# A decoder layer on one core: v is brought to token order by block transposes on VectorE and transfers through DRAM, in place of TensorE's transposes

## The chip, the cores and the metric

The kernel runs on one core of a Trainium2 chip. The metric is the device time of one execution in microseconds (us). Times are compared as medians of several runs. The engines are named as the profile names them: PE is TensorE (PEld its weight loads), DVE is VectorE, ACT is ScalarE, POOL is GpSimd, SP is SyncE, whose queue issues all of this kernel's DMAs.

## What is computed

One layer of a hybrid decoder, on a prompt of 2048 tokens of width 1024 and on 8 samples of 4 tokens. After a layer norm and a modulation, one wide projection gives u, v, z of a gated MLP, q, k, v of a gated DeltaNet with 8 heads of 128, and gates. The change is in the DeltaNet branch:

```
qkv_c, conv_new = _short_conv(qkv, conv_buf, conv_w)      # 4 taps along the tokens, then silu
q, k, v = jnp.split(qkv_c, 3, axis=-1)
q = _l2norm(q.reshape(B, L, H_B, DK)); k = _l2norm(k.reshape(B, L, H_B, DK)); v = v.reshape(B, L, H_B, DV)
...
a_mat = jnp.where(strict, einsum('bhnid,bhnjd->bhnij', kb, k) * decay, 0.0)
lhs = a_mat + jnp.eye(C)
u = triangular_solve(lhs, vb); w = triangular_solve(lhs, kb * exp(gc))
...
def step(S, xs):                                          # chunk after chunk
    v_new = u_n - w_n @ S
    o = (q_n * exp(gc_n)) @ S + qk_n @ v_new
    S = S * exp(g_last) + (k_n * exp(g_last - gc_n)).T @ v_new
```

So a head's v is needed with tokens as rows, scaled token by token, when the head's recurrence over the chunks of tokens begins.

## The kernel before

**Tiling.** The prompt runs in two halves of 1024 tokens. A projection computes 128 output columns ("group") for all tokens of a half, with channels on the 128 partitions and tokens along the free dimension: three pieces of 384, 384 and 256 + 32 sample tokens in the first half (CG[0]), two of 512 in the second (CG[1]). Each f32 operand is split into a high and a low fp32r part, so a piece is 8 x 3 matmuls on PE (project, line 906, matmuls recorded by mm at line 438). In each half come, for each of 8 heads, the groups k, q, v, z_b and for six heads a gate g_a; then the other groups.

**From a projection to the recurrence.** qkv_sink (line 1178) takes a piece of k, q or v out of PSUM into a buffer of the role "cp" (two of them, x0 the first half, y the second), does the convolution and silu, and starts k_token, q_token or v_token. These bring the piece to token order: v_token (line 1336) waits for the factor vf from k_token, transposes each chunk of 128 tokens on PE by tp (recorded at line 443) into a PSUM bank of the role "pt" (three banks), frees the buffer, and multiplies by vf on DVE into KV, the buffer of the head's k and v in token order (the tile Y4F or Y5F, by turns; tt, line 404). When all pieces are there, "vs" is signalled, for which chain (line 1523) waits.

**The inverse.** gram (line 1370) forms the products of k and q on PE. inverse (line 1412) sends their 32x32 diagonal blocks through DRAM (d_blk: four writes, four reads), POOL inverts them in 62 short steps (line 407), the result goes through DRAM again (d_td), DVE transposes 32x32 blocks (line 1446), and PE combines them to 128x128 inverses (lines 1470 to 1509). Then chain runs its eight chunks one after another, with DVE and ACT steps between its matmuls.

**What sets the order.** Every instruction is recorded by a planner (Sched): each piece of work is a generator that asks for an engine with an estimated duration and a time from which it can start; the planner takes the one with the least start plus a price by priority, and the engines run the lists in that order, each strictly in its own. A DMA is planned with 475 ns of SP and a transfer time from its bytes. The main stream of projections has the lowest priority and fills PE. A waiting instruction holds up all that stand behind it on its engine or queue. PE's weights are loaded a group or more ahead (wload, line 847).

Of the kernel before, what the change touches and what calls it, by code (L numbers as in the profile page):

```python
# [11 lines left out]
ALU = mybir.AluOpType  # L12

P = 128
D = 1024
KT = 8
H = 8
# [152 lines left out]
def hybrid_step_kernel(ctx: ExitStack, tc: tile.TileContext, x_prompt, x_sample, state_conv, state_ssm,  # L170
# [44 lines left out]
    def V(off, *dims, p0=0, np_=P):  # L215
        dims = [[1, d] if isinstance(d, int) else list(d) for d in dims]
        t, o, st = place(off)
        return bass.AP(t.tensor, t.offset + p0 * st + o, [[st, np_]] + dims)

    def Q(bank, off, *dims, p0=0, np_=P):  # L220
        dims = [[1, d] if isinstance(d, int) else list(d) for d in dims]
        return bass.AP(PS.tensor, PS.offset + p0 * 4096 + bank * 512 + off, [[4096, np_]] + dims)

    def dram(name, n):
        return dr_pool.tile([1, n], F32, name=name)[:]
# [130 lines left out]
    d_blk = [dram(f"d_blk{i}", 32 * 1024) for i in range(2)]  # L356
    d_td = [dram(f"d_td{i}", 32 * 1024) for i in range(2)]


    def fsz(ap):  # L360
        n = 1
        for s in ap.shape[1:]:
            n *= s
        return n
# [52 lines left out]
    def stt(out, a, s, b, op0, op1, dep=None):  # L417
        aps = not isinstance(s, (int, float))
        t = yield ("o", "DVE", dve_ns(out, (a, b)) + 60 * aps, dep)
        nc.vector.scalar_tensor_tensor(out=out, in0=a, scalar=s, in1=b, op0=op0, op1=op1)  # L420
        return t

    def pow_(out, a, which, dep=None):
# [17 lines left out]
    def tp(out, in_, idn=None, dep=None):  # L441
        t = yield ("o", "PE", 109.0, dep)
        nc.tensor.transpose(out, in_, ident[: in_.shape[0], : in_.shape[0]] if idn is None else idn)  # L443
        return t

    def bc(ap, shape):
        return ap.to_broadcast(shape)
# [698 lines left out]
    def hd(half, h):  # L1146
        return heads.setdefault((half, h), {})
# [30 lines left out]
    def qkv_sink(half, s, h):  # L1178
# [13 lines left out]
        def sink(cgi, pb, t):  # L1192
# [33 lines left out]
            t = yield from act(V(x0, n0), y, AF.Tanh, scale=0.5)  # L1226
            if s == 2:
                t = yield from stt(y, V(x0, n0), 1.0, y, ALU.add, ALU.mult)
                S.spawn(v_token(half, h, cgi, xb, t), 1)
            else:  # L1230
                if "KQ" not in me:
                    if "KQw" not in me:
                        me["KQw"] = True
                        kq = yield ("a", "KQ")
                        me["KQ"] = kq
                        S.signal(("KQ", half, h), kq[2])
                ta = yield ("w", ("KQ", half, h))
                dst = V(me["KQ"][0] + (0 if s == 1 else TW) + c0, n0)
                t = yield from stt(dst, V(x0, n0), 1.0, y, ALU.add, ALU.mult, dep=max(t, ta))
                S.release(xb, t)  # L1240
                S.signal(("kq", half, h, s, cgi), t)
                S.spawn(k_token(half, h, cgi, t) if s == 1 else q_token(half, h, cgi, t), 1)
# [91 lines left out]
        S.signal(("vf", half, h, cgi), t)  # L1334

    def v_token(half, h, cgi, yb, t):
        me = hd(half, h)
        ta = yield ("w", ("vf", half, h, cgi))
        cs = chunks(half, cgi)
        m, c0 = len(cs), cs[0]  # L1340
        pb = yield ("a", "pt")
        for i, c in enumerate(cs):
            t = yield from tp(Q(pb[0], i * P, P), V(yb[0] + UNIT + i * P, P), dep=max(t, pb[2]))
        S.release(yb, t)
        vf = V(me["hs"][0] + 16 + 24 + c0, m)
        t = yield from tt(V(me["KV"][0] + TW + c0 * P, [P, m], [1, P]), Q(pb[0], 0, [P, m], [1, P]),
                          bc(vf.unsqueeze(2), [P, m, P]), ALU.mult, dep=max(t, ta))
        S.release(pb, t)
        S.signal(("vs", half, h, cgi), t)

    def q_token(half, h, cgi, t):
# [951 lines left out]
```

## Time and profile before

| | us |
|---|---|
| three runs: lowest, median, highest | 2738.87, 2743.01, 2744.91 |
| the profiled execution | 2741.66 |
| its span, first to last instruction | 2739.8 |
| PE busy | 2692.0 |
| DVE, ACT, POOL busy | 1445.9, 1003.2, 553.5 |

Busy times are unions of an engine's records; matmul records overlap, since they are pipelined. A wait is put down to the instruction whose end released it. The heads of the first half run from about 130 to 760 us, those of the second from about 1480 to 2100 us.

### The profile page before, as it was taken

The numbers are of one execution on the slowest core, as the hardware profiler recorded it, in microseconds if no ns is written. First come the engines' busy times: TensorE is split into PE (matmuls) and PEld (weight loads), VectorE is DVE, ScalarE is ACT, GpSimd is POOL, SyncE is SP. The second block draws the span as 40 slices with busy tenths as digits, with TensorE's granted clock in tenths as the row PEclk, the third lists the DMA queues.
The fourth block names the chain that finished last, engine by engine and source line by source line (L and its number), as shares of the span: only waits on it lengthen the run. The fifth ranks groups of instructions, "written<-read, shape, count | busy, mean of one in ns | idle before, by whom it ended". The sixth has DMA issues, their size and how long they took to land. (4 is left out here: it accounts for less than half of the span.)

```text
span 2739.8 us, 43826 instructions
## 1 busy us (share of the span) xinstructions
PE 2692.0 (98%) x16514; PEld 2362.1 (86%) x16514; DVE 1445.9 (53%) x3194; ACT 1003.2 (37%) x2710; POOL 553.5 (20%) x1452
## 2 busy tenths in 40 slices
PE   6999999999999999999999999999999999999998
PEld 4989989998898999999997888788888888888876
DVE  5677666767552253433547655666663324433446
ACT  5544444545343322221224535444452312222120
POOL 2053444335300000000000443433341000000001
PEclk9999999999999999999999999999999999999999
DMA  6222332222553142233433222222223422233342
GB/s 213 59 70 70 84 90 63 74 69 62 152 190 95 58 125 77 86 111 92 138 109 102 79 77 69 69 61 66 77 59 92 123 95 80 71 114 104 104 124 84
DMA packets 360493, 255.88 MB, mean 93 GB/s; under 512 B 72793, under 2 KB 326033, under 8 KB 360282
## 3 DMA queue, kind: packets, MB, share of 16 engines
q1 hardware_dynamic: 360282, 253.10, 31.3%
q8 instruction: 129, 2.11, 0.3%
q14 instruction: 82, 0.67, 0.1%
HBM read 197.31 MB, written 55.71 MB: 92 GB/s over the span
## 5 line engine op out<-in xcount | busy, mean ns | idle before, releaser
L438 PE MATMUL psum<-TX,TWHL 128*128 128x384 f32 (+3 forms) x9296 | 1981.7, 361 | 3.8 <-DVE TX L404 3.4
L438 PEld LDWEIGHTS psum<-TX,TWHL 128*128 128x128 f32 (+1 forms) x9296 | 1551.8, 188 | 165.1 <-issue 10.8
L395 ACT ACTIVATE arena<-psum 128x128 bf16<-128x128 f32 (+8 forms) x920 | 311.8, 348 | 777.7 <-PE psum L438 620.8
L427 POOL TENSOR_TENSOR arena<-arena 128x1 f32<-128x1 f32 (+4 forms) x139 | 125.4, 903 | 1627.7 <-DVE arena L414 1412.2
L420 DVE SCALAR_TENSOR_TENSOR arena<-arena 128x512 f32<-128x512 f32 (+8 forms) x625 | 344.9, 561 | 92.3 <-ACT arena L395 81.0
L407 POOL TENSOR_TENSOR arena<-arena 128x60 f32<-128x60 f32 (+24 forms) x992 | 343.3, 346 | 132.7 <-DMA arena<-d_blk 26.7
L404 DVE TENSOR_TENSOR TWHL<-arena,TWHL 128x512 fp32r<-128x512 f32 (+1 forms) x344 | 235.4, 689 | 244.0 <-ACT TWHL L395 241.7
L420 DVE SCALAR_TENSOR_TENSOR arena<-arena,psum 128x128 f32<-128x128 f32 (+3 forms) x342 | 132.4, 403 | 361.2 <-PE psum L438 249.8
L395 ACT ACTIVATE TWHL<-arena 128x512 fp32r<-128x512 f32 x344 | 214.8, 627 | 206.8 <-PE psum L438 100.7
L395 ACT ACTIVATE arena<-arena 128x128 f32<-128x128 f32 (+8 forms) x509 | 228.3, 486 | 130.6 <-DVE arena L420 81.3
L443 PE MATMUL psum<-arena 128*128 128x128 f32 (+6 forms) x509 | 126.0, 271 | 2.5 <-ACT Y3F L395 0.8
L404 DVE TENSOR_TENSOR arena<-arena 128x3 f32<-128x3 f32 (+13 forms) x259 | 113.7, 447 | 18.6 <-DMA arena<-d_gc 8.7
L438 PE MATMUL psum<-arena 128*128 128x128 f32 (+6 forms) x524 | 101.6, 293 | 1.0 <-ACT arena L395 1.0
L420 DVE SCALAR_TENSOR_TENSOR arena<-psum,arena 128x512 f32<-128x512 f32 (+4 forms) x80 | 39.9, 510 | 109.8 <-PE psum L438 109.6
L1219 POOL COPY arena<-arena 128x3 f32<-128x3 f32 x120 | 35.8, 298 | 296.8 <-ACT arena L395 296.1
L438 PEld LDWEIGHTS psum<-arena 128*128 128x128 f32 (+5 forms) x524 | 73.8, 163 | 22.4 <-issue 12.7
L443 PEld LDWEIGHTS psum<-arena 128*128 128x128 f32 (+6 forms) x509 | 67.5, 137 | 26.4 <-issue 13.3
L395 ACT ACTIVATE Y7F<-psum 32x256 f32<-32x256 f32 (+6 forms) x115 | 46.6, 406 | 100.2 <-PE psum L438 39.0
L395 ACT ACTIVATE TX<-arena 128x512 fp32r<-128x512 f32 (+2 forms) x84 | 47.1, 586 | 93.1 <-DMA arena<-d_yb 75.7
L395 ACT ACTIVATION_READ_ACCUMULATOR arena<-psum 128x1 f32 (+1 forms) x392 | 76.6, 195 | 0.0
L414 DVE TENSOR_SCALAR arena<-arena 128x3 f32<-128x3 f32 (+10 forms) x234 | 47.6, 211 | 36.0 <-ACT arena L395 24.9
L404 DVE TENSOR_TENSOR TX<-arena,TX 128x512 fp32r<-128x512 f32 (+2 forms) x84 | 52.2, 638 | 24.8 <-ACT TX L395 24.4
(242 smaller groups left out, 2715.2 us busy)
## 6 DMA issues: line engine op xcount, KB each, us to landing
arena<-in_w_in_dram SPq DMA_DIRECT2D x288, 256.0 KB
out_dram<-arena SPq DMA_DIRECT2D x25, 512.0 KB
arena<-in_x_prompt_dram SPq DMA_DIRECT2D x24, 512.0 KB
arena<-d_gc SPq DMA_DIRECT2D x16, 512.0 KB
arena<-d_blk SPq DMA_DIRECT2D x64, 128.0 KB
d_yb<-arena SPq DMA_DIRECT2D x32, 256.0 KB
d_vh<-arena SPq DMA_DIRECT2D x16, 512.0 KB
arena<-d_vh SPq DMA_DIRECT2D x16, 512.0 KB
```

Source lines behind the costliest of these rows:

```text
L395: nc.scalar.activation(out, in_, func, **kw)
L404: nc.vector.tensor_tensor(out=out, in0=a, in1=b, op=op)
L407: nc.gpsimd.tensor_tensor(out=out, in0=a, in1=b, op=op)
L414: nc.vector.tensor_scalar(out=out, in0=a, scalar1=s1, scalar2=s2, op0=op0, **kw)
L420: nc.vector.scalar_tensor_tensor(out=out, in0=a, scalar=s, in1=b, op0=op0, op1=op1)
L427: nc.gpsimd.tensor_tensor(out=out, in0=a, in1=e, op=ALU.pow)
L438: nc.tensor.matmul(out, lhsT, rhs, start=start, stop=stop)
L443: nc.tensor.transpose(out, in_, ident[: in_.shape[0], : in_.shape[0]] if idn is None else idn)
L1219: nc.gpsimd.tensor_copy(V(c_tail + gi, [24, 3]), V(x0 + n0, 3))
```

## The change

v_token no longer uses PE or PSUM. DVE transposes every 32x32 block of a piece within its block of partitions (vtrans), from y back into x0. Four DMAs, one per block of 32 partitions, write the blocks to a DRAM buffer of the piece, d_v, with tokens as rows, in runs of 32 values (128 bytes). One DMA reads it back into KV in rows of 128 values. Then DVE multiplies in place by vf. The buffer "cp" is freed when the writes have landed. The read waits for the buffer KV; the wait for vf comes later than before.

```
+    d_v = {(half, h, i): dram(f"d_v{half}{h}{i}", n * P)
+           for half, ns in enumerate(((384, 384, 256), (512, 512))) for h in range(H) for i, n in enumerate(ns)}
...
+    def vtrans(out, a, dep=None):
+        t = yield ("o", "DVE", fsz(out) / 0.96 + 150, dep)
+        nc.vector.transpose(out, a)
+        return t
...
             if s == 2:
                 t = yield from stt(y, V(x0, n0), 1.0, y, ALU.add, ALU.mult)
+                t = yield from vtrans(V(x0, n0), y)
                 S.spawn(v_token(half, h, cgi, xb, t), 1)
...
     def v_token(half, h, cgi, yb, t):
         me = hd(half, h)
-        ta = yield ("w", ("vf", half, h, cgi))
         cs = chunks(half, cgi)
         m, c0 = len(cs), cs[0]
-        pb = yield ("a", "pt")
-        for i, c in enumerate(cs):
-            t = yield from tp(Q(pb[0], i * P, P), V(yb[0] + UNIT + i * P, P), dep=max(t, pb[2]))
+        dv = d_v[half, h, cgi]
+        for i in range(4):
+            t = yield from dma(DV(dv, 32 * i, [P, 32], [32 * P, 4 * m], [1, 32]),
+                               V(yb[0], [32, 4 * m], [1, 32], p0=32 * i, np_=32), dep=t)
         S.release(yb, t)
+        t = max(t, (yield ("w", ("KV", half, h))))
+        kv = V(me["KV"][0] + TW + c0 * P, [P, m], [1, P])
+        t = yield from dma(kv, DV(dv, 0, [P, P], [P * P, m], [1, P]), dep=t)
+        ta = yield ("w", ("vf", half, h, cgi))
         vf = V(me["hs"][0] + 16 + 24 + c0, m)
-        t = yield from tt(V(me["KV"][0] + TW + c0 * P, [P, m], [1, P]), Q(pb[0], 0, [P, m], [1, P]),
-                          bc(vf.unsqueeze(2), [P, m, P]), ALU.mult, dep=max(t, ta))
-        S.release(pb, t)
+        t = yield from tt(kv, kv, bc(vf.unsqueeze(2), [P, m, P]), ALU.mult, dep=max(t, ta))
         S.signal(("vs", half, h, cgi), t)
```

The planner makes new lists for all engines. Lines of the changed kernel are 3, 9 or 13 higher than those of the kernel before: 378 is 381, 404 is 407, 420 is 423, 438 is 447, 443 is 452, 1446 is 1459, 1470 is 1483.

On PE, in the last piece of the second head's v projection (first half; "128x288" are that piece's matmuls, L443 with psum<-arena the transposes of v, with Y1F those of k), before:

```order
L438 MATMUL psum<-TX,TWHL 128x384 x9
L438 MATMUL psum<-TX,TWHL 128x288 x8
L443 MATMUL psum<-arena 128x128
L438 MATMUL psum<-TX,TWHL 128x288 x4
L443 MATMUL psum<-arena 128x128
L438 MATMUL psum<-TX,TWHL 128x288 x4
L443 MATMUL psum<-arena 128x128
L438 MATMUL psum<-TX,TWHL 128x288 x8
L438 MATMUL psum<-TX,TWHL 128x384 x7
```

and now:

```order
L447 MATMUL psum<-TX,TWHL 128x288 x4
L452 MATMUL psum<-arena,Y1F 128x128
L447 MATMUL psum<-TX,TWHL 128x288 x4
L452 MATMUL psum<-arena,Y1F 128x128
L447 MATMUL psum<-TX,TWHL 128x288
L447 MATMUL psum<-arena 32x128
L447 MATMUL psum<-TX,TWHL 128x288 x10
L447 MATMUL psum<-arena 64x128
L447 MATMUL psum<-TX,TWHL 128x288 x5
L447 MATMUL psum<-TX,TWHL 128x384 x38
```

The three transposes of v are gone from between the projection's matmuls; the last two of the head's k, and two matmuls of the samples, have moved into the piece.

On SP, where the blocks of the fifth head's inverse (first half) go out and come back, before:

```order
L378 DMA arena<-in_w_in_dram 128x4x128 x2
L378 DMA d_blk_78<-Y2F 32x8x32 x4
L378 DMA arena<-d_blk_78 32x1024 x4
L378 DMA d_yb<-arena 128x512
L378 DMA arena<-in_w_in_dram 128x4x128 x2
```

and now:

```order
L381 DMA arena<-in_w_in_dram 128x4x128 x4
L381 DMA d_blk_78<-Y2F 32x8x32 x4
L381 DMA d_yb<-arena 128x32
L381 DMA d_v_94<-arena 32x12x32
L381 DMA arena<-d_blk_78 32x1024 x4
L381 DMA d_v_94<-arena 32x12x32
L381 DMA arena<-in_w_in_dram 128x4x128 x2
L381 DMA d_v_94<-arena 32x12x32
L381 DMA d_yb<-arena 128x512
L381 DMA d_v_94<-arena 32x12x32
```

A write of v, and one of the sample's result, stand between the inverse's writes and its reads, and the other three writes follow among the weight loads.

On DVE, around the first multiply of v by vf in the third head of the second half (TENSOR_TENSOR into Y4F; rows with psum and 128x128 are steps of the second head's chain), before:

```order
L404 TENSOR_TENSOR arena<-psum,arena 128x512
L420 SCALAR_TENSOR_TENSOR arena<-psum,arena,Y5F 128x128
L420 SCALAR_TENSOR_TENSOR Y6F<-Y6F,psum 128x512
L420 SCALAR_TENSOR_TENSOR arena<-arena,psum 128x128
L404 TENSOR_TENSOR Y4F<-psum,arena 128x512
L414 TENSOR_SCALAR arena<-arena 128x4
L420 SCALAR_TENSOR_TENSOR arena<-psum,arena,Y5F 128x128
```

and now:

```order
L423 SCALAR_TENSOR_TENSOR arena<-psum,arena,Y5F 128x128
L407 TENSOR_TENSOR Y0F<-Y0F,arena 128x1024
L407 TENSOR_TENSOR Y4F<-Y4F,arena 128x512
L423 SCALAR_TENSOR_TENSOR Y6F<-Y6F,psum 128x512
L423 SCALAR_TENSOR_TENSOR arena<-arena,psum 128x128
L423 SCALAR_TENSOR_TENSOR arena<-psum,arena,Y6F 128x512
L423 SCALAR_TENSOR_TENSOR arena<-psum,arena,Y5F 128x128
```

The multiply reads Y4F, which a DMA has filled, where it read PSUM; it stands later in the second head's chain, and steps of that chain stand behind it as before.

## Rows read from the trace of the kernel before

**Rows 1.** The page: the span, the engines' busy time, the DMA totals.

```profile
span 2739.8 us, 43826 instructions
PE 2692.0 (98%) x16514; PEld 2362.1 (86%) x16514; DVE 1445.9 (53%) x3194; ACT 1003.2 (37%) x2710; POOL 553.5 (20%) x1452
...
DMA packets 360493, 255.88 MB, mean 93 GB/s; under 512 B 72793, under 2 KB 326033, under 8 KB 360282
...
q1 hardware_dynamic: 360282, 253.10, 31.3%
```

**Rows 2.** Busy time by stage: each engine's us (instructions), PE clock, DMA share.

```profile
130.00:760.00 630.00, 626.45 (x4704) 569.37 (x4703) 428.55 (x1125) 294.45 (x993) 267.44 (x713) 1.00 0.30 83
...
1480.00:2100.00 620.00, 617.00 (x3874) 502.21 (x3873) 372.81 (x745) 283.48 (x828) 231.33 (x622) 1.00 0.26 71
```

**Rows 3.** PE in order of time: start, us from start to last end, instructions.

```profile
170.30 1.23 PE L438 MATMUL psum<-TX,TWHL 128*128 128x288 f32 x8
171.37 0.27 PE L443 MATMUL psum<-arena 128*128 128x128 f32 x1
171.39 0.78 PE L438 MATMUL psum<-TX,TWHL 128*128 128x288 f32 x4
172.01 0.27 PE L443 MATMUL psum<-arena 128*128 128x128 f32 x1
172.04 0.77 PE L438 MATMUL psum<-TX,TWHL 128*128 128x288 f32 x4
```

**Rows 4.** DVE's groups by shape: busy us, mean ns, idle before.

```profile
L1446 DVE STREAM_TRANSPOSE arena<-arena 128x256 f32<-128x256 f32 x16 | 7.0, 438 | 8.8 <-DMA arena<-d_td 8.8
...
L404 DVE TENSOR_TENSOR Y4F<-psum,arena 128x512 f32<-128x512 f32 x16 | 11.0, 686 | 2.0 <-PE psum L443 1.9
...
L404 DVE TENSOR_TENSOR arena<-arena 128x512 f32<-128x512 f32 x24 | 16.6, 690 | 0.7
...
L404 DVE TENSOR_TENSOR Y4F<-psum,arena 128x384 f32<-128x384 f32 x16 | 8.7, 550 | 0.1
```

**Rows 5.** SP's issues by tile: least/median/longest ns, first and last start.

```profile
L378 SPq DMA_DIRECT2D d_blk<-Y2F x32: 303/446/457, 129.3 to 1967.1; - x32
...
L378 SPq DMA_DIRECT2D arena<-in_w_in_dram x296: 367/428/2573, 21.2 to 2420.9; - x148
```

**Rows 6.** SP in order of time, the third head's blocks.

```profile
271.92 1.82 SPq L378 DMA_DIRECT2D d_blk<-Y2F  x4
275.00 1.70 SPq L378 DMA_DIRECT2D arena<-d_blk  x4
```

**Rows 7.** Busy time while these four writes move; DMA share last but one.

```profile
272.30:274.90 2.60, 2.60 (x20) 2.55 (x20) 0.98 (x5) 1.45 (x8) 0.00 (x0) 1.00 0.35 51
```

**Rows 8.** POOL's steps of an inverse, and DVE beside the last, in order of time.

```profile
456.80 0.68 POOL L407 TENSOR_TENSOR arena<-arena 128x63 f32<-128x63 f32 x2
465.60 0.63 POOL L407 TENSOR_TENSOR arena<-arena 128x65 f32<-128x65 f32 x1
...
464.62 1.45 DVE L404 TENSOR_TENSOR TWHL<-arena,TWHL 128x512 fp32r<-128x512 f32 x2 [0.18 <-ACT TWHL L395]
```

**Rows 9.** Slack: DVE's transpose and PE's start, in two inverses, by time.

```profile
742.59 0.45 DVE L1446 STREAM_TRANSPOSE arena<-arena 128x256 f32<-128x256 f32 x1 [5.05 <-DMA arena<-d_td]
...
744.22 0.35 PE L1470 MATMUL psum<-arena,Y3F 32*32 32x32 f32 x10
...
2081.38 0.45 DVE L1446 STREAM_TRANSPOSE arena<-arena 128x256 f32<-128x256 f32 x1 [3.75 <-DMA arena<-d_td]
...
2085.18 0.41 PE L1470 MATMUL psum<-arena,Y3F 32*32 32x32 f32 x14
```

**Rows 10.** DVE's waits: total us, times, longest.

```profile
DVE arena L404 <- DMA arena<-d_gc: 8.7, 7, 2.0
```

**Rows 11.** PE's waits for steps of the inverse, the same columns.

```profile
PE psum L1470 <- DVE arena L1446: 1.7, 2, 1.4
PE psum L1479 <- DVE Y7F L414: 1.1, 3, 0.5
PE psum L1476 <- ACT Y7F L395: 1.1, 1, 1.1
```

## The prediction

> **What bounds the kernel now.** I read the page first, then the busy time by stage, PE's own waits, and last PE's instructions in order of time. The page gives PE 2692.0 of 2739.8 us, 98% [rows 1]: the other engines are at 53% and less. The 47.8 us in which PE is not busy are mostly the start (the first 55 us). In the two stages in which the sixteen heads run (eight in each half of the tokens) PE is busy 626.45 of 630 us and 617.00 of 620 us, at the full clock of 2.4 GHz (PEclk 1.00), beside a DVE at 68% and 60%, a POOL at 42% and 37% and DMA engines at 30% and 26% [rows 2]. So here PE's list of work is the time, and a change counts by what it takes off that list, less what it makes PE wait.
>
> A busy share alone could mislead, since matmul records overlap. So I measure PE by the ends of its records, in a piece that holds three of the transposes in question [rows 3]. Eight projection matmuls of 288 columns end at 170.30 + 1.23 = 171.53; the transpose behind them ends at 171.37 + 0.27 = 171.64; four more matmuls end at 172.17; the next transpose at 172.28; four more at 172.81. The matmuls go on at 0.53 / 4 = 0.13 us each, and each transpose moves everything behind it by 0.11 us, not by its record's 0.27. The 0.11 is the price on the path.
>
> **What the change takes off PE.** v has 16 chunks of 128 tokens in each of 8 heads: 128 transposes. 128 x 0.11 = 14.1 us (from 0.10 to 0.12, the rounding of these rows: 12.8 to 15.4). Nothing is added to PE's list. A page puts another figure beside this: the Trainium skill, VectorE: DVE Perf Modes, The three transpose paths, gives 390 ns for a 128x128 transpose on TensorE, and its Rules for kernel authors advise TensorE for 128x128 where PSUM may hold the result, which speaks against this change. By 390 ns the gain would be 50 us and the time 2692 us. The ends in [rows 3] say 110 ns in a stream of other matmuls; the trace decides, and 14.1 stands.
>
> **What it adds to DVE.** 40 block transposes: per head three in the first half of the tokens (384, 384, 256 columns), two of 512 in the second. One of 256 columns took 438 ns; DVE's cost per further column is (686 - 550) / 128 = 1.06 ns, from its 384- and 512-column multiplies [rows 4]. So 574 and 710 ns: 8 x (2 x 574 + 438) + 16 x 710 = 24.0 us. The 40 multiplies by the factor vf remain, now from SBUF instead of PSUM: 690 ns against 686 at 512 columns [rows 4], no difference. DVE has 201 idle us in the first stage of heads and 247 in the second [rows 2], so I cost the 24 us at nothing; if none of it were covered, the gain would be gone and 10 us more.
>
> **What it adds to SP's queue and the DMA engines.** Per piece of v four writes of 32 partitions and one read: 160 writes and 40 reads. The nearest write is that of the blocks of the inverse, 32 partitions x 8 blocks of 128 bytes: 446 ns of SP; a read of 512-byte rows is like a weight load: 428 ns [rows 5]. v's writes have 8, 12 or 16 blocks (32, 64 and 64 of them). If an issue costs the same whatever its size, SP gets 160 x 0.446 + 40 x 0.428 = 88 us more; if it grows with the blocks, 32 x 0.446 + 64 x 0.669 + 64 x 0.892 + 17 = 131 us. Either is under 11% of the 1250 us of these stages. I take the first, by the nearer row. On the engines: the four inverse writes, 1024 blocks, took a share of 0.35 over 2.60 us [rows 7] = 0.91 us; v's 65,536 blocks make 64 times that, 58 us, and its 8.4 MB back some 28 us at the page's mean (31.3% of 2739.8 us for 255.88 MB, 3.35 us a MB [rows 1]). 86 us over 1250 raise the share from 0.3 to under 0.4. At nothing again, while transfers that PE waits for aren't queued behind them.
>
> Which are those? The inverse of each head: its blocks go out by d_blk, POOL runs 62 short steps, the result comes back by d_td, DVE transposes it (L1446), PE starts (L1470). The order puts at most one write of v between a head's d_blk writes and reads, as in the fourth fence of the part on the change. SP stands idle there anyway: the four writes are issued by 273.74, the reads go at 275.00, when the writes have landed [rows 6]. A write of 0.45 us fits into those 1.26 us.
>
> **What it adds as waits.** (a) The four writes wait for the transpose, the read for the writes' landing; behind the read on SP stand weight loads, d_blk and d_td. (b) The multiply waits on DVE for the read; behind it stand steps of the previous head's chain over its chunks, for which PE waits (last two fences). The nearest row is d_gc, also read back from DRAM for DVE: 7 of its 16 reads came late, 8.7 us in all [rows 10], 0.54 us a read. For 40 reads: between 0 and 21.8 us of DVE's time, some of it PE's. I take 0, because DVE's idle time is over 30% and v is wanted only when the head's inverse is done; the upper end goes to a rival. (c) The conv buffer "cp" is held until the writes land. v is the last of a head's three users, and the z_b and mostly the ga projections stand between it and the next: nothing, or one landing of 1.7 us if not.
>
> **POOL against DVE.** POOL's steps of 63 columns take 0.68 / 2 = 0.34 us with the gap between them, and one of 65 took 0.63 while DVE worked on two SBUF operands from 464.62 to 466.07 [rows 8]: 0.3 us more for a collision. v's multiply had one operand in PSUM and now has both in SBUF, so each can cost the running inverse 0.3 us: three or two per head, at most 1.0 us. The Trainium skill, SBUF — State Buffer, Who interferes with whom, says that a DVE instruction with two SBUF inputs shuts out a GpSimd one that reads SBUF for its whole length; the row shows the same in kind. By the whole length, 3 x 0.55 us, the delay would be 1.7 us instead of 1.0 and the time 2733 us.
>
> What does a later inverse cost? PE's start has slack. In the last head of the first half DVE's transpose ends at 743.04 and PE starts at 744.22: 1.2 us, the smallest; in the last head of all 2081.83 and 2085.18: 3.35 us, the largest [rows 9]. Fourteen lie between; in two PE already waits, 1.7 us in all [rows 11]. With slack spread evenly over these 2.15 us, a delay of d us costs PE 2 d + 14 (d - 1.2)^2 / 4.3 (the second part from d = 1.2). For d = 1.0: **2.0 us**.
>
> **The sum.** 14.1 - 2.0 = 12.1 us off. The profiled execution took 2741.66 us, its span 2739.8, 1.35 us below the median of the three runs, 2743.01. 2741.66 - 12.1 = 2729.6, and 2731 on the median's scale.
>
> **Rivals.**
> 1. More: PE's waits for steps of the inverse are 1.7 + 1.1 + 1.1 us [rows 11]. The new order may meet them better, and the transposes' PSUM banks come free earlier. 14.1 + 3.9 = 18.0 off: 2725. Against it: POOL's collisions go the other way.
> 2. The gain is waited away. A landing on SP (0.45 us of issue and 1.26 of waiting [rows 6]) comes ahead of each head's d_blk or d_td besides the collisions: d = 2.7, cost 5.4 + 7.3 = 12.7, net 1.4 off: 2742, no change. For it: in three heads the order has a read of v directly ahead of the d_blk writes. Against: in thirteen it hasn't.
> 3. Slower: DVE, strictly in order, stands at the multiply for the read each time, as at d_gc, and PE waits along: 21.8 + 2.0 - 14.1 = 9.7 on: 2753. It decides from (14.1 - 2.0) / 40 = 0.30 us a read, if all of it reaches PE. For it: [rows 10] is the same kind of load, issued by the same plan. Against: much of DVE's wait falls into its idle time.
>
> **How the numbers follow.** The forecast, 2726 to 2737, has 0.60; more, 0.10; waited away, 0.17; slower, 0.13. A measurement of this kernel can tell about 0.2%, 5.5 us, from no change, so faster means under 2737.5: 0.60 + 0.10 less a little of the forecast's upper edge, 0.69; same 0.18; slower 0.13. The range takes in the rival with more, the rounding of the 14.1, and the waited-away case with some us above it: 2724 to 2746.
>
> **What would show it.** PE's matmuls fall by 128 to 16,386, and its busy time by about 14 us. PE's waits for L1446 (by its new line) stay under 4 us in all; POOL's loop of each head is longer by under 1 us. DVE's waits for reads of d_v show up as a row: under 5 us in all for the forecast, 20 for rival 3. SP's waits on writes of d_v are many and cost nothing. The prediction is wrong if PE's busy time falls by the 14 us and the span doesn't: then the new rows among PE's waits say which of rivals 2 and 3 it was. It is wrong in its main term if the busy time falls by much less or more than 14.

## The result: 2722.5 us, 0.7% faster

| | before, us | changed, us |
|---|---|---|
| median, first series (6 runs each) | 2741.97 | 2722.50 |
| ratio, 95% interval | | 0.9932, 0.9919 to 0.9944 |
| the changed kernel measured again (9 and 5 runs) | 2743.69 | 2724.19, ratio 0.9928, 0.9914 to 0.9942 |
| the profiled execution, its span | 2741.66, 2739.8 | 2721.62, 2719.9 |
| PE busy, PE idle within the span | 2692.0, 47.8 | 2676.6, 43.3 |

The direction was right, but the time lies 1.5 us below the range, and the gain of 19.5 us is 1.6 times the 12.1 that were forecast. The page of the changed kernel, to be read against [rows 1]:

```profile
span 2719.9 us, 44021 instructions
PE 2676.6 (98%) x16386; PEld 2351.3 (86%) x16386; DVE 1467.0 (54%) x3234; ACT 1002.8 (37%) x2710; POOL 557.0 (20%) x1452
...
q1 hardware_dynamic: 445402, 269.89, 34.6%
```

PE has its 128 matmuls fewer and 15.4 us less busy time; another 4.5 us of the 19.9 by which the span is shorter were PE's idle time. The two stages of the heads, to be read against [rows 2]:

```profile
130.00:760.00 630.00, 629.26 (x4713) 574.39 (x4712) 440.55 (x1148) 295.08 (x996) 265.52 (x714) 1.00 0.37 96
...
1480.00:2100.00 620.00, 618.89 (x3885) 507.29 (x3884) 381.53 (x767) 285.80 (x840) 237.87 (x620) 1.00 0.33 86
```

PE is busier than before (629.26 of 630, 618.89 of 620), and DMA has risen from 0.30 to 0.37 and from 0.26 to 0.33. So where did PE's waits go? These are all that are left in its list of waits for the lines of the inverse (1483 to 1522 now):

```profile
PE psum L1520 <- ACT Y7F L398: 0.3, 1, 0.3
...
PE psum L1509 <- ACT Y7F L398: 0.2, 1, 0.2
```

The three rows of [rows 11], 3.9 us, are gone.

**PE's list, record by record.** Give each of PE's records the time from the end of the record before it to its own end, as the prediction did for [rows 3], and add these up by kind from the first projection matmul to PE's last record. What comes before is left out, since it took from 49.0 to 54.4 us in the profiled executions with the same work in it (the medians contain it), and the work adds up without overlap. The table has all kernels of this study (the last two columns are the projections' matmuls and the other ones); it is worked out from their traces.

| kernel | matmuls | sum, us | transposes | inverse | projections | other |
|---|---|---|---|---|---|---|
| before | 16514 | 2680.6 | 105.0 | 45.8 | 2252.3 | 277.5 |
| changed | 16386 | 2661.0 | 88.8 | 40.5 | 2251.6 | 280.1 |
| changed, again | 16386 | 2660.6 | 88.6 | 40.7 | 2252.1 | 279.2 |
| transposes back | 16514 | 2676.0 | 104.7 | 41.6 | 2251.5 | 278.2 |
| no transfers | 16386 | 2659.8 | 90.7 | 42.2 | 2249.9 | 277.0 |
| before, later inverse | 16514 | 2672.9 | 103.5 | 41.0 | 2251.2 | 277.1 |
| changed, later inverse | 16386 | 2659.1 | 89.3 | 40.2 | 2250.9 | 278.7 |
| changed, earlier inverse | 16386 | 2675.6 | 90.7 | 48.7 | 2254.6 | 281.7 |
| multiply on ACT | 16386 | 2663.8 | 90.4 | 41.1 | 2251.1 | 281.3 |
| v from KV | 16386 | 2659.5 | 87.9 | 41.3 | 2250.8 | 279.5 |
| k too, first half | 16322 | 2659.9 | 81.5 | 41.0 | 2253.7 | 283.7 |
| the same, later inverse | 16322 | 2654.2 | 80.4 | 41.8 | 2252.3 | 279.7 |
| k too, both halves | 16258 | 2702.3 | 81.5 | 39.7 | 2280.9 | 300.1 |

Of the 19.6 us between the first two rows, 16.2 are the transposes and 5.3 the inverse's matmuls, less 1.9 elsewhere. The second execution of the changed kernel comes to the same within 0.4 us.

**Why the inverse's waits went.** One of the two tight heads, its DVE transpose and what PE does then, in order of time; before:

```profile
1727.83 0.43 DVE L1446 STREAM_TRANSPOSE arena<-arena 128x256 f32<-128x256 f32 x1
```

```profile
1725.21 1.79 PE L438 MATMUL psum<-TX,TWHL 128*128 128x512 f32 x7
1728.41 0.69 PE L1470 MATMUL psum<-arena,Y2F 32*32 32x32 f32 x32 [1.41 <-DVE arena L1446]
```

and in the changed kernel:

```profile
1715.65 0.44 DVE L1459 STREAM_TRANSPOSE arena<-arena 128x256 f32<-128x256 f32 x1
```

```profile
1715.79 1.13 PE L447 MATMUL psum<-Y1F 128*128 128x256 f32 x4 [0.42 <-DVE Y1F L423]
1716.75 0.27 PE L452 MATMUL psum<-arena,Y1F 128*128 128x128 f32 x1
1716.96 0.63 PE L1483 MATMUL psum<-arena,Y2F 32*32 32x32 f32 x28
```

Before, PE had run out of work at 1727.00 and stood idle for 1.41 us, until 0.15 us after the transpose's end. Now it still has four matmuls and a transpose to do and comes 0.87 us after that end. That is the smallest slack of the 16 heads now; before, the smallest two were 0.05 and 0.15. The table shows where this comes from: "work" is what PE's list holds between a head's last gram matmul and the inverse's first, by the order of the instructions and the median interval of each kind (an estimate); "path" goes from the head's first d_blk write to the end of DVE's transpose; "slack" from there to PE's start; all are means of 16 heads. The waits are those of the line of L1470.

| kernel | work | path | slack, least | PE's waits |
|---|---|---|---|---|
| before | 57.7 | 55.5 | 1.80, 0.05 | 1.7 (2) |
| changed | 58.6 | 55.7 | 2.23, 0.87 | 0 |
| transposes back | 58.2 | 55.1 | 2.42, 0.15 | 1.0 (1) |
| no transfers | 57.5 | 55.0 | 2.11, 0.83 | 0 |
| before, later inverse | 61.1 | 58.0 | 2.29, 1.01 | 0 |
| changed, later inverse | 61.3 | 58.4 | 2.53, 1.44 | 0 |
| changed, earlier inverse | 56.2 | 54.7 | 1.23, 0.05 | 3.5 (3) |

The change made the path 0.3 us longer, as a mean, and the planner's new list put 0.9 us more work ahead of it. In the head shown it is 54.4 us before and 58.0 now. The mean does not decide: the kernel without transfers has 57.5 us and no such wait. What counts is the tightest heads, which each new list lays out anew.

**What such a wait costs besides.** Busy time, granted clock and DMA share of PE's worst place of the kernel before, the inverse of the last head of the first half, in windows of 1 us (the same columns as [rows 2]):

```profile
747.00:748.00 1.00, 0.57 (x4) 0.25 (x2) 0.57 (x1) 0.43 (x1) 0.00 (x0) 1.00 0.13 39
748.00:749.00 1.00, 0.24 (x2) 0.13 (x2) 0.74 (x2) 0.95 (x3) 0.00 (x0) 1.00 0.05 10
749.00:750.00 1.00, 0.56 (x46) 0.56 (x46) 0.80 (x2) 0.12 (x1) 0.00 (x0) 1.00 0.00 0
750.00:751.00 1.00, 1.00 (x19) 0.92 (x9) 0.42 (x1) 0.31 (x1) 0.00 (x0) 0.90 0.15 46
751.00:752.00 1.00, 1.00 (x9) 0.56 (x10) 0.29 (x1) 0.44 (x2) 0.00 (x0) 0.50 0.95 316
...
753.00:754.00 1.00, 1.00 (x5) 0.91 (x5) 0.00 (x0) 0.25 (x1) 0.00 (x0) 0.50 0.00 0
754.00:755.00 1.00, 1.00 (x15) 0.75 (x14) 0.00 (x0) 0.59 (x2) 0.00 (x0) 0.89 0.00 0
```

PE is idle for 1.6 us of the first three windows: it waits at L1476 for ACT and at L1479 for DVE [rows 11]. Then the granted clock falls from 1.00 to 0.50, from 2.4 to 1.2 GHz, and is back at 1.00 soon after 754: some 3.4 us in which all of PE's work takes twice as long, 1.7 us lost. The changed kernel has the full clock in this stretch.

This wait is not a matter of the work ahead of L1470, where the head has 1.2 us of slack [rows 9]. It comes from ACT's list. Between L1470 and L1476 ACT has to copy the result (Y7F<-psum), and before the change this copy stood behind two conversions of weights (TWHL), which waited for their weights from DRAM:

```profile
744.22 0.69 PE L1470 MATMUL psum<-arena,Y3F 32*32 32x32 f32 x32
...
746.21 0.63 ACT L395 ACTIVATE TWHL<-arena 128x512 fp32r<-128x512 f32 x1 [2.76 <-DMA arena<-in_w_in_dram]
747.57 0.63 ACT L395 ACTIVATE TWHL<-arena 128x512 fp32r<-128x512 f32 x1 [0.73 <-DMA arena<-in_w_in_dram]
748.23 0.38 ACT L395 ACTIVATE Y7F<-psum 32x256 f32<-32x256 f32 x1
```

In the changed kernel ACT's new list has the copy ahead of the next conversions:

```profile
733.57 0.69 PE L1483 MATMUL psum<-arena,Y3F 32*32 32x32 f32 x32
...
734.29 0.38 ACT L398 ACTIVATE Y7F<-psum 32x256 f32<-32x256 f32 x1 [1.74 <-PE psum L1483]
734.88 1.41 ACT L398 ACTIVATE TWHL<-arena 128x512 fp32r<-128x512 f32 x2 [0.21 <-DMA arena<-in_w_in_dram]
```

The copy ends 3.7 us after L1470's matmuls before, and 0.4 us after L1483's now.

I had read PEclk 1.00 for the whole stage in [rows 2] and stopped there; as a mean over 630 us it rounds the fall away.

**The other steps.** DVE's new and changed groups by shape, in the columns of [rows 4]:

```profile
L429 DVE STREAM_TRANSPOSE arena<-arena 128x512 f32<-128x512 f32 x16 | 11.3, 708 | 0.3
...
L429 DVE STREAM_TRANSPOSE arena<-arena 128x384 f32<-128x384 f32 x16 | 9.1, 569 | 0.0
...
L407 DVE TENSOR_TENSOR Y4F<-Y4F,arena 128x512 f32<-128x512 f32 x8 | 5.6, 702 | 0.8 <-DMA Y4F<-d_v 0.7
...
L429 DVE STREAM_TRANSPOSE arena<-arena 128x256 f32<-128x256 f32 x8 | 3.5, 439 | 0.1
```

and DVE's waits for the reads of v:

```profile
DVE Y5F L407 <- DMA Y5F<-d_v: 1.5, 3, 0.8
DVE Y4F L407 <- DMA Y4F<-d_v: 1.1, 2, 0.7
```

The transposes took 708, 569 and 439 ns (710, 574 and 438 forecast). Five of 40 multiplies waited for their read, 2.6 us in all. SP, where the third head's blocks leave and come back, to be read against [rows 6]:

```profile
277.64 1.79 SPq L381 DMA_DIRECT2D d_blk<-Y2F  x4
279.47 0.45 SPq L381 DMA_DIRECT2D d_v<-arena  x1
282.49 1.71 SPq L381 DMA_DIRECT2D arena<-d_blk  x4
```

The write of v takes its 0.45 us, but the reads now go 3.06 us after the writes are issued (279.43 to 282.49), where they went after 1.26. As a mean of 16 heads the reads stand 4.56 us behind the first write, 3.36 before. Of these 1.2 us, POOL's loop with what lies around it (from the reads to d_td's first write, 42.28 instead of 42.99 us) and d_td's way (8.90 instead of 9.11) gave back 0.9.

### The profile page after: what moved, and what is told of

It is laid out like the page before. It is cut to its first block, busy times and chain, and to the rows that moved or that the text cites. A ratio compares the mean times of both kernels' runs of the same rounds, so it can differ in the third digit from the quotient of the medians.

```text
span 2719.9 us, 44021 instructions
## 1 busy us (share of the span) xinstructions
PE 2676.6 (98%) x16386; PEld 2351.3 (86%) x16386; DVE 1467.0 (54%) x3234; ACT 1002.8 (37%) x2710; POOL 557.0 (20%) x1452
## 4 chain that ended last, share of the span: by engine, by line
PE 95%; DMA 2%; DVE 1%; ACT 1%; issue 0%; SPq 0%; POOL 0%; POOLq 0%; ACTq 0%; DVEq 0%
PE psum L447 90%; PE psum L452 3%; DMA arena<-in_w_o_dram 0%; ACT arena L398 0%; DMA arena<-in_w_in_dram 0%; PE psum L1483 0%; PE psum L1509 0%; PE psum L1520 0%; DVE arena L730 0%; DMA arena<-in_state_ssm_dram 0%; DVE arena L732 0%; PE psum L1489 0%; DVE arena L423 0%; PE psum L650 0%; DMA Y0F<-in_x_prompt_dram 0%
## 5 line engine op out<-in xcount | busy, mean ns | idle before, releaser
L398 ACT ACTIVATE arena<-psum 128x128 bf16<-128x128 f32 (+10 forms) x920 | 311.8, 348 | 769.9 <-PE psum L447 587.9
L436 POOL TENSOR_TENSOR arena<-arena 128x4 f32<-128x4 f32 (+4 forms) x139 | 120.1, 865 | 1598.3 <-DVE arena L417 1388.7
L410 POOL TENSOR_TENSOR arena<-arena 128x60 f32<-128x60 f32 (+24 forms) x992 | 358.6, 361 | 169.6 <-DMA d_v<-arena 57.5
L398 ACT ACTIVATE arena<-arena 128x128 f32<-128x128 f32 (+9 forms) x509 | 229.4, 486 | 118.2 <-DVE arena L423 81.8
L407 DVE TENSOR_TENSOR arena<-arena 128x1024 f32<-128x1024 f32 (+13 forms) x259 | 114.3, 446 | 15.0 <-DMA arena<-in_lnv_g_dram 4.9
L447 PE MATMUL psum<-arena 128*128 128x128 f32 (+8 forms) x524 | 102.3, 293 | 1.2 <-ACT arena L398 1.0
L452 PE MATMUL psum<-arena 128*128 128x128 f32 (+7 forms) x381 | 93.2, 269 | 3.4 <-ACT TX L398 1.5
L398 ACT ACTIVATION_READ_ACCUMULATOR arena<-psum 128x1 f32 x392 | 76.6, 195 | 0.0
L452 PEld LDWEIGHTS psum<-arena 128*128 128x128 f32 (+7 forms) x381 | 49.9, 136 | 23.0 <-issue 11.9
L417 DVE TENSOR_SCALAR arena<-arena 128x3 f32<-128x3 f32 (+10 forms) x234 | 47.8, 209 | 34.0 <-ACT arena L398 25.8
```

The costliest lines, as they stand in the source:

```text
L398: nc.scalar.activation(out, in_, func, **kw)
L407: nc.vector.tensor_tensor(out=out, in0=a, in1=b, op=op)
L410: nc.gpsimd.tensor_tensor(out=out, in0=a, in1=b, op=op)
L417: nc.vector.tensor_scalar(out=out, in0=a, scalar1=s1, scalar2=s2, op0=op0, **kw)
L436: nc.gpsimd.tensor_tensor(out=out, in0=a, in1=e, op=ALU.pow)
L447: nc.tensor.matmul(out, lhsT, rhs, start=start, stop=stop)
```

## The experiments

Theory A says: PE's list is the time; the transposes cost it their 0.11 us each and a little waiting, and the rest of the gain is PE's waits for the inverse, which the new lists avoid. Theory B says: the transposes cost more than their 0.11 us. Theory C: the new transfers or collisions still hold PE up. Every kernel was timed against the kernel before on the same chip.

| kernel | median, us | before beside it | ratio, 95% interval |
|---|---|---|---|
| transposes back | 2737.66 | 2742.30 | 0.9984, 0.9976 to 0.9993 |
| no transfers | 2727.01 | 2742.30 | 0.9943, 0.9928 to 0.9958 |
| before, later inverse | 2736.80 | 2742.30 | 0.9980, 0.9969 to 0.9991 |
| changed, later inverse | 2720.61 | 2742.30 | 0.9924, 0.9909 to 0.9939 |
| changed, earlier inverse | 2738.45 | 2743.24 | 0.9980, 0.9969 to 0.9991 |
| multiply on ACT | 2727.28 | 2743.24 | 0.9936, 0.9924 to 0.9949 |
| k too, first half | 2721.36 | 2743.24 | 0.9919, 0.9905 to 0.9932 |
| k too, both halves | 2760.62 | 2743.24 | 1.0058, 1.0042 to 1.0073 |
| the first-half one, later inverse | 2715.06 | 2743.69 | 0.9897, 0.9883 to 0.9910 |
| v from KV | 2726.02 | 2743.69 | 0.9931, 0.9917 to 0.9945 |
| changed, again | 2724.19 | 2743.69 | 0.9928, 0.9914 to 0.9942 |

**Transposes back.** In the changed kernel's v_token:

```diff
-        S.release(yb, t)
+        pb = yield ("a", "pt")
+        tq = 0.0
+        for i in range(m):
+            tq = yield from tp(Q(pb[0], i * P, P), V(yb[0] + UNIT + i * P, P), dep=max(tq, pb[2]))
+        S.release(pb, tq)
+        S.release(yb, max(t, tq))
```

> The changed kernel, with v's 128 PE transposes put back beside the new path: each piece's chunks are transposed on PE into a pt bank that nobody reads and that is free again when PE is done. Theory A (price and slack): a transpose costs PE its 0.11 us and a little waiting, 14 to 15.5 us in all, and the other 3 to 5 us of the gain were PE's waits for the inverse, which vanished because the new list has more PE work ahead of L1470: 2736.5 to 2738, and PE's waits for the inverse stay under 2 us. Theory B (the transposes themselves cost more than their 0.11 us, through weight loads, banks or the matmuls behind them): all of the gain goes, 18.6 us or more, 2741 or above.

2737.66 us, within theory A's 2736.5 to 2738 and below B's 2741. PE's busy time is that of the kernel before again, within some 2 us, and one wait for the inverse's first matmul (now L1488) is left:

```profile
PE 2694.1 (98%) x16514; PEld 2364.1 (86%) x16514; DVE 1469.1 (54%) x3234; ACT 1004.5 (37%) x2710; POOL 554.9 (20%) x1452
```

```profile
PE psum L1488 <- DVE arena L1464: 1.0, 1, 1.0
```

In PE's list the 128 transposes make 2676.0 - 2661.0 = 15.0 us, 0.117 each. With all of the new path's cost on board and no transpose saved, the kernel is still 4.6 us faster than before (ratio 0.9984, up to 0.9993): that part of the gain isn't the transposes'.

**No transfers.** The writes and the read are taken out, and the multiply reads the buffer cp, so v is not brought to token order:

```diff
-        for i in range(4):
-            t = yield from dma(DV(dv, 32 * i, [P, 32], [32 * P, 4 * m], [1, 32]),
-                               V(yb[0], [32, 4 * m], [1, 32], p0=32 * i, np_=32), dep=t)
...
-        t = yield from dma(kv, DV(dv, 0, [P, P], [P * P, m], [1, P]), dep=t)
...
-        t = yield from tt(kv, kv, bc(vf.unsqueeze(2), [P, m, P]), ALU.mult, dep=max(t, ta))
+        t = yield from tt(kv, V(yb[0], [P, m], [1, P]), bc(vf.unsqueeze(2), [P, m, P]), ALU.mult, dep=max(t, ta))
+        S.release(yb, t)
```

> The changed kernel without the 160 writes and 40 reads of d_v: the multiply by vf takes v from the buffer cp. Left out: v is not brought to token order, only each 32x32 block is transposed. Theory A: the transfers cost PE nothing; its list has no more work ahead of the inverse than the kernel before (57.5 us between the last gram and the inverse's first matmul, by the median prices of PE's instructions; 57.7 before, 58.6 in the changed kernel), so the 14 to 15.5 us of the transposes are gained, and some of PE's waits for the inverse are back: 2724 to 2728. Theory C (the transfers hold something up that PE waits for): faster than the changed kernel by 3 us or more, under 2719.5. Theory B: 18.6 us off 2742 as in the changed kernel, 2722 to 2724, with no waits for the inverse.

2727.01 us, in theory A's range and above C's 2719.5. In its one profiled execution PE's list comes to 2659.8 us, 1.2 less than in the changed kernel. The 200 transfers cost PE between nothing and 1.2 us. The waits for the inverse that were expected back are there only in part: none at its first matmuls, 0.9 and 0.8 us at two later steps (L1504, L1515). Its median is 4.5 us above the changed kernel's, its list isn't: the profiled execution (2720.73 us) had a mean granted clock of 0.998, and four of the six had 0.994 to 0.996. So the place of the median in theory A's range says little.

**Before and changed, with the inverse later.** One number of the planner, in either kernel:

```diff
-        tw = yield from dma(V(Uc, [32, 8], [1, 32]), DV(dt_, 0, [32, P], [4096, 8], [1, 32]), dep=tw)
+        tw = yield from dma(V(Uc, [32, 8], [1, 32]), DV(dt_, 0, [32, P], [4096, 8], [1, 32]), dep=tw, late=2000.0)
```

> The kernel before, with one number of the planner changed: it takes d_td's read to land 2.0 us later, so that the inverse's matmuls stand later in PE's list (61.1 us of work ahead of them instead of 57.7). Nothing else of the program is changed. Theory A: the 4.6 us of PE's waits for the inverse (L1470, L1476, L1479, L1507) vanish without the change of v: 2736.5 to 2739, 3 to 5.5 us faster than before. Theory B: these waits don't carry the gain: 2741 to 2743.

> The changed kernel with the same number of the planner changed (61.3 us of PE work ahead of the inverse's matmuls instead of 58.6). Theory A: PE's waits for the inverse are gone already, so nothing more is to be had: 2721 to 2724. If the shorter slack of the changed kernel still cost something that the waits don't show: 2719 or less. If a later inverse makes the chains late, 2725 or more.

The kernel before becomes 5.5 us faster by that number alone: 2736.80, within theory A's 2736.5 to 2739. The waits for L1470 are gone; these are what is left of the inverse's:

```profile
PE psum L1479 <- DVE Y7F L414: 0.6, 1, 0.6
...
PE psum L1507 <- ACT Y7F L395: 0.3, 1, 0.3
```

The changed kernel gains little more, 2720.61 (2721 to 2724 expected). Between the two, with the waits for the inverse's first matmuls out of the way in both, PE's lists differ by 2672.9 - 2659.1 = 13.8 us, 0.108 us for each of 128 transposes. That is the forecast's 14.1; their medians differ by 16.2. The table above has a detail worth keeping: of the 3.4 us of work put ahead of the matmuls in the kernel before, only 0.5 became slack, since the planner moved DVE's transpose back in DVE's list too (path 58.0 us instead of 55.5).

**Changed, with the inverse earlier.** The same number, -2000.

> The changed kernel with one number of the planner changed: it takes d_td's read to land 2.0 us earlier than it plans now, so that the inverse's matmuls stand earlier in PE's list: 56.2 us of PE work between the last gram and them (mean of 16 heads), where the changed kernel has 58.6. Nothing else of the program is changed. Theory A (PE's slack before the inverse carries a quarter of the gain): head by head, the slack of the changed kernel less the work taken away leaves PE waiting in nine heads, some 10 us at the inverse's first matmuls, and less if the waits shift one another: 2727 to 2733, with a row of 4 to 11 us for the wait of L1483 on L1459. Rival (PE's waits for the inverse are unconnected with where it stands): 2721 to 2724, no such row.

2738.45 us, 16 us above the changed kernel's median (13 by the ratios of the two), where 5 to 10 were expected. Theory A has the direction and the rival is out (2721 to 2724), but the sum of the waits was not as expected: three heads wait at L1483, not nine, 3.5 us in all.

```profile
PE psum L1483 <- DVE arena L1459: 3.5, 3, 2.3
```

PE's list is 14.6 us longer, and over half of this is again the clock. Around the longest wait, in windows of 1 us:

```profile
2011.00:2012.00 1.00, 0.19 (x1) 0.00 (x0) 0.00 (x0) 0.84 (x2) 0.19 (x1) 1.00 0.08 14
2012.00:2013.00 1.00, 0.00 (x0) 0.00 (x0) 0.00 (x0) 0.00 (x0) 0.00 (x0) 1.00 0.75 117
2013.00:2014.00 1.00, 0.46 (x18) 0.47 (x20) 0.96 (x2) 0.00 (x0) 0.00 (x0) 0.64 0.00 0
2014.00:2015.00 1.00, 1.00 (x25) 0.94 (x20) 1.00 (x2) 0.37 (x1) 0.00 (x0) 0.50 0.00 0
...
2023.00:2024.00 1.00, 1.00 (x16) 0.86 (x13) 0.00 (x0) 0.30 (x2) 0.00 (x0) 0.74 0.06 16
```

PE is idle for 2.35 us and then runs at 1.2 GHz for over 10 us. A second wait, 2.09 us at 147.8 in the first head (for DVE's Y1F, not for the inverse), is followed by another fall. In windows of 20 us:

```profile
140.00:160.00 20.00, 17.91 (x92) 15.89 (x92) 10.66 (x31) 10.34 (x35) 8.79 (x27) 0.83 0.45 119
2000.00:2020.00 20.00, 17.65 (x144) 13.57 (x143) 14.96 (x35) 9.03 (x28) 8.63 (x17) 0.83 0.09 14
2020.00:2040.00 20.00, 20.00 (x125) 16.35 (x124) 12.63 (x26) 7.52 (x22) 4.74 (x17) 0.91 0.42 94
```

20 x (0.17 + 0.17 + 0.09) = 8.6 us of full-speed work lost, besides 3.5 + 2.1 = 5.6 us of these waits themselves.

**Multiply on ACT.** One ACT instruction per chunk in place of the DVE multiply:

```diff
-        t = yield from tt(kv, kv, bc(vf.unsqueeze(2), [P, m, P]), ALU.mult, dep=max(t, ta))
+        t = max(t, ta)
+        for i, c in enumerate(cs):
+            kc = V(me["KV"][0] + TW + c * P, P)
+            t = yield from act(kc, kc, AF.Copy, scale=V(me["hs"][0] + 16 + 24 + c, 1), dep=t)
```

> The changed kernel with the multiply of v by vf on ACT (one instruction per chunk with vf as its scale) instead of DVE, so that it has no DVE instruction with two SBUF operands beside POOL's steps. If the collisions delay the inverse by up to 1.0 us a head, as the prediction put it, the 16 loops on POOL get shorter by 5 us or more in all; by what the trace of the changed kernel shows (12 us of the multiplies lie beside POOL's steps and slow them by about half of that time) by 4 to 8 us. The time follows only if PE waits there: 2720 to 2725 by theory A, since it doesn't; under 2718 if the collisions cost PE anything that the waits hide.

POOL's steps, before, changed, and here (count | busy us, mean ns | idle before):

```profile
L407 POOL TENSOR_TENSOR arena<-arena 128x60 f32<-128x60 f32 (+24 forms) x992 | 343.3, 346 | 132.7 <-DMA arena<-d_blk 26.7 <-PE psum L438 18.4 <-DVE arena L1428 12.4
```

```profile
L410 POOL TENSOR_TENSOR arena<-arena 128x60 f32<-128x60 f32 (+24 forms) x992 | 358.6, 361 | 169.6 <-DMA d_v<-arena 57.5 <-PE psum L447 13.9 <-DMA arena<-d_blk 12.7
```

```profile
L410 POOL TENSOR_TENSOR arena<-arena 128x60 f32<-128x60 f32 (+24 forms) x992 | 341.2, 344 | 159.3 <-DMA d_v<-arena 30.9 <-DVE arena L1444 23.4 <-DVE TWHL L407 17.4
```

The collision is real: with v's multiply on DVE, from SBUF, the steps take 15.3 us more in all, 0.96 us a head, and without it they take what they took before. The multiply itself accounts for less than half of this: it lies beside the steps for some 12 us, and a least-squares fit of the time from step to step to what DVE did meanwhile gives a delay of about 0.55 us for each of them, some 6.5 us in all or 0.4 us a head. DVE's other instructions with two SBUF operands lie beside the steps for 134 us in the changed kernel and for 124 before, by the new lists, and at the same price that would be most of the rest (an estimate). Nor did the loops follow: the 16 loops, from first step to last, are 591.7 us before, 583.3 changed, 589.1 here: the expectation of loops 4 to 8 us shorter failed. The time from one step's end to the next one's is 423 ns before, 438 changed and 424 here where one follows the other directly; what POOL does and waits for between the other steps outweighs that, and why it was less in the changed kernel isn't settled. The time, 2727.28 us, is 2 us above the range expected. ACT's multiply is no gain.

**k the same way, and a faster version.** In the first half only, with v's block transposes in KV too; then with the inverse later; then v alone from KV; and k in both halves on the changed kernel. The core of k's edit:

```diff
-        for i, c in enumerate(cs):
-            t = yield from tp(Q(pb[0], i * P, P), V(me["KQ"][0] + c * P, P), dep=max(t, pb[2]))
...
+        ko = me["KV"][0] + c0 * P
+        t = yield from vtrans(V(ko, m * P), V(me["KQ"][0] + c0 * P, m * P), dep=max(t, ta))
+        for i in range(4):
+            t = yield from dma(DV(dk, 32 * i, [P, 32], [32 * P, 4 * m], [1, 32]),
+                               V(ko, [32, 4 * m], [1, 32], p0=32 * i, np_=32), dep=t)
...
+        te = yield from dma(kv, DV(dk, 0, [P, P], [P * P, m], [1, P]), dep=t)
```

> A version meant to be faster than both: v's block transposes go into the head's buffer KV, from where they are written out and into which they are read back, so the buffer cp is free after the transpose; in the first half of the tokens k takes the same way (64 PE transposes fewer); and the planner takes transfers in runs of 128 bytes at half its price. Theory A: 64 transposes at 0.12 us, 7.7 us off the changed kernel, less some waits for the inverse that come back, since its list has 56.4 us of PE work ahead of the inverse instead of 58.6: 2714 to 2721. Rival (k comes later to gram, so the inverse and the chain are late, and PE waits): 2724 or more.

> The changed kernel with k brought to the order of tokens in the same way as v, in both halves (block transpose on DVE into KV, four writes, one read): 128 PE transposes fewer. Simple view (each transpose off PE's list is 0.12 us, as with v): 2706 to 2709. Rival (the way through DRAM takes some 17 us from the block transpose to the multiply in the changed kernel; v isn't wanted before the chain, but k's factor is wanted by gram, so the inverse and the chain begin later, the head keeps its two-fold buffers longer, and PE has no work left): slower than the changed kernel by 25 to 70 us, 2747 to 2793, most of it in the second half, where a head has fewer groups of projections beside it.

> The version with k in the first half of the tokens on the way through DRAM too (as in the earlier run) and with d_td's read planned 2.0 us later, so that 59.4 us of PE work stand ahead of the inverse's matmuls instead of 56.4. If PE's waits around the inverse took back what 64 transposes fewer should give: 2711 to 2717. If k's late arrival takes it back (waits for gram and the chain, not for the inverse): 2719 to 2724, no better than the changed kernel.

> The changed kernel with v's block transposes in the head's buffer KV instead of cp, the transfers in runs of 128 bytes planned at half their price, and d_td's read planned 2.0 us later; k as before on PE. 58.9 us of PE work ahead of the inverse, as in the changed kernel (58.6). PE's list is that of the changed kernel and no wait of size is left: 2719 to 2723. Under 2717 if the buffer cp, held until the writes land, cost something in the changed kernel.

> The changed kernel once more, to see how its list runs a second time: 2720 to 2725; PE busy 15 to 16 us under that of the kernel before, no wait of PE for the inverse's first matmuls, and no fall of the granted clock between 130 and 1450 us, if these are properties of its list and not of one execution.

In both halves it is slower: 2760.62 us, 38 more than the changed kernel, with 128 matmuls fewer. v has time to take the way through DRAM, k hasn't. That the reason is gram, which needs k's factor, is argued and not shown: PE's longest waits between 1480 and 2180 us stand further on:

```profile
PE psum L449 <- ACT arena L400: 10.6, 16, 2.1
PE psum L449 <- ACT Y0R L400: 9.0, 1, 9.0
PE psum L454 <- DVE arena L409: 5.1, 3, 3.7
```

These are steps of the chains and the end of the stage. The clock adds to them: it falls in five stretches in which the changed kernel has none, some 54 us at 0.50 in all, the longest from 2150 to 2180. PE is busy for 37 us of these, and half of that, some 19 of the 38 us, is an estimate of what the clock took. In the first half, where a head has more projections beside it, k's way is hidden: 2721.36 us at first, just past the end of the range, with nothing gained: 64 transposes fewer, 7.3 us, but 3.6 and 2.1 us more at the other matmuls and the projections; with the inverse later 2715.06, within the 2711 to 2717 expected. That is the fastest kernel here, 0.9897 of the kernel before (0.9883 to 0.9910), and its PE list is 6.8 us below the changed kernel's. v from KV (inverse later and, as in both first-half kernels, transfers in short runs planned at half their price) gives 2726.02, above the 2719 to 2723 expected, with PE's list at 2659.5 us, 1.5 below the changed kernel's: holding cp cost nothing of size. The changed kernel again gave what was expected: no wait for the inverse's first matmuls and no fall of the clock between 130 and 1450 us.

## Why the prediction was half right

- **PE's list bounds the kernel: right.** The gain lies where PE's list or its waits got shorter, and nowhere else.
- **128 transposes, 14.1 us: right.** 13.8 us where no waits disturb (the two later-inverse kernels), 15.0 when put back, 16.2 in the table, which has the few waits of PE at transposes in it. The 390 ns that the Trainium skill gives for one, in bf16 (VectorE: DVE Perf Modes, The three transpose paths), are not the price in a stream of matmuls here: 0.108 to 0.127 us is.
- **DVE's 24.0 us and the multiplies at nothing: right.** 23.9 us measured, DVE waits 2.6 us for the reads. Rival 3, with its 21.8 us of such waits, fell.
- **SP and DMA at nothing: right in the sum, wrong in one step.** "A write of 0.45 us fits into those 1.26 us" did not hold: the reads of the inverse's blocks went 1.2 us later as a mean. It cost nothing, since PE had more to do by then.
- **POOL's collisions, up to 1.0 us a head: right as a bound, wrong in effect.** The steps take 0.96 us more a head, some 0.4 of it by v's multiply, but the loops did not get longer, and the whole path only 0.3 us. The Trainium skill (SBUF — State Buffer, SBUF: two separate sides) has a DVE instruction with two SBUF inputs and a GpSimd one that reads SBUF shut each other out, the second for the whole length of the first. The size measured here doesn't agree with that: the multiply delayed the steps by about 0.55 us for each us beside them, and the measurement decides.
- **"What does a later inverse cost", + 2.0 us: wrong, and this is the step that failed.** I took the slack of the 16 heads from the trace of before and only added a delay to it. But the slack is not a property of the inverse; it is what the planner's lists put ahead of a wait, and the change makes new lists for all engines. The term came out at -5.3 instead of +2.0. The waits at L1470, 1.7 us, which I held fixed, went away, and so did 2.4 of 2.9 us at the inverse's later steps (1.1, 1.1 and 0.7 before; 0.3 and 0.2 now), for which the term had no place; part of the rest is the clock's. The orders of the two kernels lay open: counting the PE work between gram and L1470 gives 57.7 us before and 58.6 now, and 54.4 and 58.0 in the head that waited longest; and in ACT's list the copy that L1476 waits for stood behind two conversions and now stands ahead of them.
- **That the new lists were the better ones was luck.** Nothing in the change aims at them, and they could have come out worse: the first list with k on the same way has 56.4 us of work ahead of the inverse.
- **The clock, not in the sum at all.** 1.7 us of the profiled execution before went to the fall of the clock at 750 us behind a wait. Rival 1 named the right mechanism (waits of [rows 11] that the new order may avoid) and the right size within 3 us, 2725; I gave it 0.10, because I let POOL's collisions speak against it.

## What to carry to other kernels

Where a planner lays out the order, the slack ahead of each wait belongs to the list and not to the work: count it in the new lists, of all engines, for the tight places before adding a delay to the old one, and try one number of the planner on the kernel before to see what the list alone is worth (5.5 us here, over a quarter of this gain). A transpose can leave TensorE by a slow way through DRAM if its result has time: v had, k had in the half with more work beside it and not in the other. A short wait of a busy TensorE should be priced with what the clock does after it.

## What was not expected of the hardware

The granted clock fell to 0.50 after waits in the middle of a stretch in which PE was otherwise full: after 1.6 us of idle time spread over 2.4 us, with 32x32 matmuls of the inverse between (some 3.4 us at half speed), and after idle stretches of 2.35 and about 2 us (10 and nearly 7 us at half speed). So a wait cost, with the work lost behind it, up to about three times its length. It did not fall after each one: the wait of 1.41 us at 1728 in the kernel before left the clock at 1.00. What decides between them, the runs here don't tell. One more fall, of 3.4 to 6.8 us between 1454 and 1478, is in every kernel of this study, before and changed alike.
